# Rows of the second expert table gathered as 4 tokens x 32 slots, and summed by 32-column matmuls

## The chip, the cores and the metric

The kernel runs on one core of one Trainium2 chip. The metric is the device time of one execution in microseconds, as the median of several runs. Three runs of the kernel before gave 2932.99, 2933.3 and 2942.21 us, so the median is 2933.3 us.

## The reference, cut to what matters

The program computes three transformer blocks on one sequence of 256 tokens with 2048 channels, in 32-bit floating point. The change touches only one part, the expert layer at the end of the first block. For every token it picks 8 heads x 16 = 128 experts out of 16384, takes a dot product of the token with each expert's row of `expert_u`, and adds up the same experts' rows of `expert_v` with the resulting weights:

```
s1 = einsum('thd,nd->thn', q[:, :, 0], sk[0]); s2 = einsum(... q[:, :, 1], sk[1])
v1, i1 = top_k(s1, 16);  v2, i2 = top_k(s2, 16)
cs, ci = top_k(v1[..., :, None] + v2[..., None, :], 16)      # per token and head
experts = row * 128 + col;  gates = softmax(cs)
a = gelu(einsum('chkd,cd->chk', expert_u[experts], h))
out = einsum('chk,chkd->cd', gates * a, expert_v[experts])   # 128 rows per token
```

One row of either table is 2048 floats, 8 KB. 256 tokens x 128 experts x 2 tables are 65,536 rows, 512 MiB.

## The kernel before

Tokens lie on the 128 partitions, in two tiles t = 0 and 1. Outside the expert layer the program is a series of dense layers (`dense`): weights come in parts of 512 KB on SP's queue (`raw<-...`), ScalarE makes the high part of the split weight (`hi`, L110), VectorE the low part (`lo`, L111), and TensorE runs three matmuls per part and token tile (L178 to L180). `prep` keeps three parts (`LOOK`) ready ahead. ACT stands for ScalarE, DVE for VectorE, PE for TensorE, POOL for GpSimd and SP for SyncE.

The expert layer (`peer`) starts with the dense layer `w_qp`, 4 column blocks. After each block, `ev_qp` makes scores, and `route` finds the 16 best per head for two heads, that is 32 of the 128 expert slots of a token tile. It is some 40 small DVE instructions, written as a generator that runs a piece at each tick of the program. It ends with a cast of 32 expert numbers into `eidx` (L696). The four routes of t = 0 run inside and right behind `w_qp`; the scores of t = 1 wait in `sc1`, and its four routes (`late`) run beside the gathers.

Gathers are indirect DMAs that POOL issues (L740). One gather brings, for one slot k, the rows of 128 tokens, one on each partition: 128 x 8 KB = 1 MiB. Five buffers of that size go round: four of `gslot` and one in `hj`. The order written out by hand is a pair for each slot, first the u row, then the v row. In `step`, DVE takes the dot product of the u row with the tokens (L788, two instructions, 128x2048) and the buffer is free; ACT applies gelu and the gate (L790, L791). One slot later `vsum` uses the v row: ACT makes a diagonal matrix of the weights (`dg`, L764), PE multiplies it with the first 1024 columns of the row (L766, two matmuls of 512 columns, which the trace counts as four records of two passes each), and DVE adds the other 1024 columns, scaled, to `xres` (L767, "the half-sum"). When the 128 slots of a token tile are through, DVE adds the two PSUM accumulators to `xres` (L774), and `after_v` squares, transposes and splits the rows for the next layer, `ev_in`. Its first four weight parts are asked for 12 slots before the end.

Every 32-bit float matmul of 512 columns in this layer is two records on PE, each with a weight load of its own (PEld).

## Time and profile before

| what | value |
|---|---|
| median of three runs | 2933.3 us |
| the profiled execution | 2928.4 us, of which its span 2926.7 us |
| PE busy | 2349.1 us, 80% of the span |
| DVE busy | 1992.8 us, 68% |
| ACT, POOL busy | 1024.9 us (35%), 613.4 us (21%) |
| granted PE clock, mean | 0.876 of full speed |
| moved by gathers (queue software_dynamic) | 543.62 MB of 820.08 MB |
| gather stage, from the first gather to the last landing | 716.6 us to 2097.8 us |

The profiled execution's time is its span and 1.7 us around it. The page divides the span into 40 equal slices of 73 us; the stage of the gathers fills slices 10 to 28. Times within the program are counted from the start of the span. A queue or an engine is read as the bound of a stretch where it is busy throughout and the others wait for it.

### The profile page before, as it was taken

How to read it: one execution, taken by the hardware profiler on the slowest of the kernel's cores; microseconds unless marked ns; L12 is line 12 of the kernel's file. 1: busy time of each engine (PE TensorE's matmuls, PEld its weight loads, DVE VectorE, ACT ScalarE, POOL GpSimd, SP SyncE). 2: the span in 40 equal slices, each digit the busy share in tenths (PEclk: the TensorE clock that was granted, in tenths of full speed). 3: DMA queues.
4: the chain of work that ended last, by engine and by line, in shares of the span. 5: the costliest groups of instructions: out<-in, count | busy, mean ns of one | idle time of the engine just before them, and what ended most of it. 6: DMA issues, size and time to landing. Idle time of an engine off the chain costs nothing.

```text
span 2926.7 us, 25901 instructions
## 1 busy us (share of the span) xinstructions
PE 2349.1 (80%) x8448; PEld 1541.0 (53%) x8448; DVE 1992.8 (68%) x2705; ACT 1024.9 (35%) x1984; POOL 613.4 (21%) x569
## 2 busy tenths in 40 slices
PE   9999999999855555556655556565699999999999
PEld 7878888887511111111211111111388888888887
DVE  5665755657999767766766676667765566577754
ACT  6544544444422111111211111111344444446553
POOL 0000000000333444444444444444300000000000
PEclk9999999999965767786787677867899999999999
DMA  7545466556999999999999999999865555554345
GB/s 251 171 143 186 152 219 198 185 188 226 368 331 325 415 396 419 415 400 394 391 412 404 397 415 406 404 402 416 327 195 189 169 170 189 188 174 130 123 155 168
DMA packets 151912, 820.08 MB, mean 280 GB/s; under 512 B 17217, under 2 KB 17249, under 8 KB 85729
## 3 DMA queue, kind: packets, MB, share of 16 engines
q0 software_dynamic: 75312, 543.62, 46.6%
q1 hardware_dynamic: 76464, 274.81, 28.6%
q8 instruction: 67, 1.10, 0.2%
q14 instruction: 69, 0.56, 0.1%
HBM read 816.26 MB, written 2.10 MB: 280 GB/s over the span
## 4 chain that ended last, share of the span: by engine, by line
PE 48%; issue 18%; DMA 17%; POOL 8%; DVE 7%; ACT 1%; POOLq 0%; SPq 0%; DVEq 0%; ACTq 0%
PE acc L178 14%; PE acc L180 14%; PE acc L179 14%; DMA gslot<-expert_u,eidx 10%; POOL gslot L740 6%; DMA hj<-expert_u,eidx 5%; POOL hj L740 2%; DVE hj L788 2%; PE tr L207 1%; DVE lo L111 1%; DVE xres L767 1%; PE sd L1060 1%; PE sd L1069 1%; PE tr L284 1%; DMA xt<-xT 0%
## 5 line engine op out<-in xcount | busy, mean ns | idle before, releaser
L766 PE MATMUL acc<-gslot,dg 128*128 128x512 f32 x1024 | 769.8, 894 | 556.7 <-ACT dg L764 539.1
L111 DVE TENSOR_TENSOR lo<-raw,hi 128x1024 fp32r<-128x1024 f32 (+1 forms) x516 | 622.8, 1210 | 465.6 <-ACT hi L110 465.2
L766 PEld LDWEIGHTS acc<-gslot,dg 128*128 128x128 f32 x1024 | 242.1, 260 | 1075.8 <-ACT dg L764 873.6
L110 ACT ACTIVATE hi<-raw 128x1024 fp32r<-128x1024 f32 (+1 forms) x516 | 541.1, 1049 | 703.4 <-PE acc L180 628.3
L178 PE MATMUL acc<-hi,h 128*128 128x512 f32 (+1 forms) x1472 | 583.5, 397 | 3.7 <-ACT hi L110 3.3
L179 PE MATMUL acc<-lo,h 128*128 128x512 f32 (+1 forms) x1472 | 574.7, 390 | 4.5 <-DVE lo L111 4.5
L180 PE MATMUL acc<-hi,h 128*128 128x512 f32 (+1 forms) x1472 | 574.2, 390 | 0.8 <-DVE h L217 0.8
L767 DVE SCALAR_TENSOR_TENSOR xres<-gslot,wsl,xres 128x1024 f32<-128x1024 f32 x256 | 328.4, 1283 | 139.3 <-ACT wsl L791 125.6
L790 ACT ACTIVATE wsl<-dots 128x1 f32<-128x1 f32 x256 | 51.9, 203 | 1050.0 <-DVE dots L788 1050.0
L788 DVE CUSTOM_DVE_ANT_0 hj<-gslot,hj 128x2048 f16<-128x2048 f32 x129 | 295.5, 2291 | 111.6 <-DMA gslot<-expert_u,eidx 111.6
L788 DVE CUSTOM_DVE_ANT_0 hj<-hj 128x2048 f16<-128x2048 f32 x127 | 290.9, 2291 | 100.6 <-DMA hj<-expert_u,eidx 100.6
L740 POOL DMA_INDIRECT gslot<-expert_v,eidx x256 | 320.2, 1251 | 92.7 <-issue 75.8
L178 PEld LDWEIGHTS acc<-hi,h 128*128 128x128 f32 x1472 | 277.0, 188 | 67.4 <-issue 7.9
L179 PEld LDWEIGHTS acc<-lo,h 128*128 128x128 f32 x1472 | 277.5, 189 | 62.9 <-DVE lo L111 7.0
L180 PEld LDWEIGHTS acc<-hi,h 128*128 128x128 f32 x1472 | 277.2, 188 | 60.0 <-issue 1.6
L740 POOL DMA_INDIRECT gslot<-expert_u,eidx x129 | 127.8, 990 | 417.5 <-DVE dots L788 331.1
L195 POOL TENSOR_TENSOR rs_y<-rs_v,mhalf 128x2 f32<-128x2 f32 (+2 forms) x25 | 28.0, 1121 | 803.8 <-DVE rs_v L194 803.2
L740 POOL DMA_INDIRECT hj<-expert_u,eidx x127 | 123.1, 969 | 345.1 <-DVE dots L788 314.3
L764 ACT ACTIVATE dg<-ident,wsl 128x128 f32<-128x128 f32 x256 | 102.7, 401 | 8.4
L791 ACT ACTIVATE wsl<-wsl,gate 128x1 f32<-128x1 f32 x256 | 75.3, 294 | 8.2
L270 ACT ACTIVATE at<-at,sm_nm 128x128 f32<-128x128 f32 (+1 forms) x112 | 49.6, 444 | 40.4 <-DVE sm_nm L263 22.1
L178 PE MATMUL acc<-hi,mT 128*128 128x512 f32 x128 | 50.1, 392 | 0.0
(287 smaller groups left out, 2152.4 us busy)
## 6 DMA issues: line engine op xcount, KB each, us to landing
raw<-ev_in SPq DMA_DIRECT2D x128, 512.0 KB, 4.5
raw<-od_in SPq DMA_DIRECT2D x72, 512.0 KB, 3.8
raw<-w_gate SPq DMA_DIRECT2D x64, 512.0 KB, 4.0
raw<-w_dqkv SPq DMA_DIRECT2D x48, 512.0 KB, 3.6
raw<-w_out SPq DMA_DIRECT2D x32, 512.0 KB, 3.9
raw<-w_qp SPq DMA_DIRECT2D x32, 512.0 KB, 5.3
raw<-ev_out SPq DMA_DIRECT2D x32, 512.0 KB, 4.1
raw<-od_out SPq DMA_DIRECT2D x32, 512.0 KB, 4.4
```

The costliest lines, as they stand in the source:

```text
L110: nc.scalar.activation(hi, raw, AF.Copy)
L111: nc.vector.tensor_tensor(lo, raw, hi.bitcast(F32), op=ALU.subtract)
L178: nc.tensor.matmul(o, xh, wh, start=(k == 0), stop=False)
L179: nc.tensor.matmul(o, xh, wl, start=False, stop=False)
L180: nc.tensor.matmul(o, xl, wh, start=False, stop=(k == kc * kk - 1))
L740: nc.gpsimd.indirect_dma_start(out=g, out_offset=None, in_=d[table], in_offset=bass.IndirectOffsetOnAxis(ap=eidx[:, t, k:k + 1], axis=0))
L764: nc.scalar.activation(dg, self.ident, AF.Copy, scale=w)
L766: nc.tensor.matmul(st["acc"][n], dg, g[:, n * 512:(n + 1) * 512], start=(k == 0), stop=(k == P - 1))
L767: nc.vector.scalar_tensor_tensor(xres[:, t, VPE:], g[:, VPE:], w, xres[:, t, VPE:], op0=ALU.mult, op1=ALU.add)
L788: nc.vector.tensor_tensor_reduce(junk, gu, hrow[:, t], 1.0, 0.0, op0=ALU.mult, op1=ALU.add, accum_out=dots[:, t, o])
L790: nc.scalar.activation(wsl[:, t, o], dots[:, t, o], AF.Gelu_apprx_tanh)
L791: nc.scalar.activation(wsl[:, t, o], wsl[:, t, o], AF.Copy, scale=gate[:, t, o])
```

## The change

It replaces the way in which v rows are fetched, weighted and summed; u rows are fetched and used as before.

- A v gather now brings 4 tokens x 32 slots of one route block: partition 32m + r holds slot r of token 4i + m of a group q of 32 tokens. 32 such gathers cover the 128 tokens of a block. `spread` brings the expert numbers into that layout (`eidv`): a transpose on PE and four 32x32 casts on DVE, in each route.
- When 32 u slots are done, `weights` computes gelu and gate for all of them at once, transposes the weights with `spread`, and multiplies them with a constant mask into `lw`, 32 matrices of 128x32. So a v row needs four matmuls of 512 columns with 32 weight columns each, whose result goes to 32 of the 128 partitions of four PSUM accumulators. The diagonal, the half-sum and ACT's work for each slot are gone. `use_v` handles two v rows at a time.
- v rows run 36 places behind u rows (`VLAG`). The list of gathers begins with 36 u rows, goes on with u and v in turn, and ends with v rows alone.
- The two split-weight buffers `hi` and `lo` are one pool `hlp` of four buffers of 1 MiB. After `w_qp` all four also hold gathered rows (`hg`); within the last 16 uses they are given back, and only then are the first weight parts of `ev_in` asked for. One of the four `gslot` buffers holds the scores of t = 1 until they are routed. So four buffers go round at first, eight after `w_qp`, nine at the end.

```diff
-VPE = 1024
+VLAG = 36
...
-        self.hip = pool("hip", 4)
-        self.lop = pool("lop", 4)
+        self.hlp = pool("hlp", 4)
...
-        while self.nprep < min(upto, len(self.plan)):
+        while self.nprep < min(upto, self.limit, len(self.plan)):
             src, ks, n = self.plan[self.nprep]
             raw = self.rawp.tile([P, ks, n], F32, tag="raw", name="raw")
             nc.sync.dma_start(raw, src)
-            hi = self.hip.tile([P, ks, n], F32R, tag="hi", name="hi")
-            lo = self.lop.tile([P, ks, n], F32R, tag="lo", name="lo")
+            hl = self.hlp.tile([P, 2, ks, n], F32R, tag="hl", name="hl")
+            hi, lo = hl[:, 0], hl[:, 1]
...
-        base = [gslot[:, i] for i in range(4)] + [gbc]
-        free = deque(base)
-        ready = [[0, 0], [0, 0]]
+        sc1 = gslot[:, 3].rearrange("p (b c) -> p b c", b=4)
+        free = deque([(gslot[:, i], False) for i in range(3)] + [(gbc, False)])
+        ready = [0, 0]
...
+        def spread(dst, src, b, copy):
+            tp = self.tr()
+            nc.tensor.transpose(tp[:, :P], src, self.ident)
+            tv = tp[32 * b:32 * b + 32, :P].rearrange("p (i m) -> p m i", m=4)
+            for m in range(4):
+                copy(dst[32 * m:32 * m + 32], tv[:, m])
...
+            spread(eidv[:, t, sl], ef[:, t], b, nc.vector.tensor_copy)
...
+        seq = []
+        for j in range(256 + VLAG):
+            if j < 256:
+                seq.append(("u", j))
+            if j >= VLAG:
+                seq.append(("v", j - VLAG))
+        st = {"issue": 0, "use": 0, "acc": None, "keep": True, "gone": 0}
+        held, lws, pair = {}, {}, []
+
+        def vpos(v):
+            t, b, r = v // P, v // 32 % 4, v % 32
+            return t, b, r // 4, r % 4
...
+                kind, j = seq[st["issue"]]
+                if kind == "u":
+                    t, k = j // P, j % P
+                    if k >= ready[t]:
+                        return
+                    table, ix = "expert_u", eidx[:, t, k:k + 1]
+                else:
+                    t, b, i, q = vpos(j)
+                    c = 32 * b + 8 * q + i
+                    table, ix = "expert_v", eidv[:, t, c:c + 1]
+                g = free.popleft()
+                nc.gpsimd.indirect_dma_start(out=g[0], out_offset=None, in_=d[table],
+                                             in_offset=bass.IndirectOffsetOnAxis(ap=ix, axis=0))
+                held[kind, j] = g
...
-        def vsum(i, g):
-            t, k = todo[i]
-            w = wsl[:, t, k:k + 1]
-            if k == 0:
-                st["acc"] = [self.acc() for _ in range(2)]
-            dg = dgp.tile([P, P], F32, tag="dg", name="dg")
-            nc.scalar.activation(dg, self.ident, AF.Copy, scale=w)
-            for n in range(2):
-                nc.tensor.matmul(st["acc"][n], dg, g[:, n * 512:(n + 1) * 512], start=(k == 0), stop=(k == P - 1))
-            nc.vector.scalar_tensor_tensor(xres[:, t, VPE:], g[:, VPE:], w, xres[:, t, VPE:], op0=ALU.mult, op1=ALU.add)
-            free.append(g)
...
+        def weights(t, b):
+            sl = slice(32 * b, 32 * b + 32)
+            nc.scalar.activation(dots[:, t, sl], dots[:, t, sl], AF.Gelu_apprx_tanh)
+            nc.vector.tensor_tensor(dots[:, t, sl], dots[:, t, sl], gate[:, t, sl], op=ALU.mult)
+            yield 1
+            wT = self.small(32, "wT", bufs=2)
+            spread(wT, dots[:, t], b, lambda o, i: nc.scalar.activation(o, i, AF.Copy))
+            lw = pp.tile([P, 4, 8, 32], F32, tag="lw", name="lw", bufs=2)
+            nc.vector.tensor_tensor(lw, vmask.unsqueeze(1).to_broadcast([P, 4, 8, 32]),
+                                    wT.rearrange("p (g i) -> p g i", g=4).unsqueeze(3).to_broadcast([P, 4, 8, 32]), op=ALU.mult)
+            lws[t, b] = lw
...
+        def use_u(j):
+            t, k = j // P, j % P
+            g = held.pop(("u", j))
+            nc.vector.tensor_tensor_reduce(junk, g[0], hrow[:, t], 1.0, 0.0, op0=ALU.mult, op1=ALU.add,
+                                           accum_out=dots[:, t, k:k + 1])
+            give(g)
+            if k % 32 == 31:
+                self.spawn(weights(t, k // 32))
+
+        def use_v(v):
+            pair.append(v)
+            if len(pair) < 2:
+                return
+            gs = [held.pop(("v", x)) for x in pair]
+            if v % P == 1:
+                st["acc"] = [self.acc() for _ in range(4)]
+            for n in range(4):
+                for x, g in zip(pair, gs):
+                    t, b, i, q = vpos(x)
+                    nc.tensor.matmul(st["acc"][n][32 * q:32 * q + 32], lws[t, b][:, q, i], g[0][:, n * 512:(n + 1) * 512],
+                                     start=(x % P < 4), stop=(x % P >= P - 4))
+            pair.clear()
+            for g in gs:
+                give(g)
...
+            while st["use"] < len(seq):
+                kind, j = seq[st["use"]]
+                if (kind, j) not in held or (kind == "v" and vpos(j)[:2] not in lws):
+                    return
+                (use_u if kind == "u" else use_v)(j)
+                st["use"] += 1
+                fill()
+                if kind == "v" or j < VLAG:
+                    return
...
+        for _ in range(4):
+            free.append((self.hlp.tile([P, D], F32, tag="hl", name="hg"), True))
...
+            if st["keep"] and st["use"] >= len(seq) - 16:
+                st["keep"] = False
+                for g in [g for g in free if g[1]]:
+                    free.remove(g)
+                    st["gone"] += 1
+            if st["gone"] == 4:
+                st["gone"] = 0
+                self.limit = len(self.plan)
                 self.prep(self.ncons + 1 + LOOK)
```

In PE's program, in the middle of the stage of t = 0, `dg` is a slot's diagonal, `lw` a block's weight table; each row is one matmul of 512 columns, and the buffers of `gslot` all have one number. Before:

```order
L766 MATMUL acc_5891<-gslot_5352,dg_7546 128x512
L766 MATMUL acc_5892<-gslot_5352,dg_7546 128x512
L766 MATMUL acc_5891<-gslot_5352,dg_7556 128x512
L766 MATMUL acc_5892<-gslot_5352,dg_7556 128x512
L766 MATMUL acc_5891<-gslot_5352,dg_7566 128x512
L766 MATMUL acc_5892<-gslot_5352,dg_7566 128x512
L766 MATMUL acc_5891<-gslot_5352,dg_7576 128x512
L766 MATMUL acc_5892<-gslot_5352,dg_7576 128x512
```

And of the changed kernel, at the same place:

```order
L815 MATMUL acc_6317<-hg_5981,lw_6635 32x512
L815 MATMUL acc_6318<-hg_5981,lw_6635 32x512
L815 MATMUL acc_6319<-hg_5981,lw_6635 32x512
L815 MATMUL acc_6320<-hg_5981,lw_6635 32x512
L664 MATMUL tr_6864<-ident_84,dots_5119 128x128
L815 MATMUL acc_6317<-hg_5983,lw_6635 32x512
L815 MATMUL acc_6318<-hg_5983,lw_6635 32x512
L815 MATMUL acc_6319<-hg_5983,lw_6635 32x512
L815 MATMUL acc_6320<-hg_5983,lw_6635 32x512
```

Where two matmuls of a v row stood, four stand now, one after another on the same buffer (`hg_5981`, then `hg_5983`), and those of the next row follow. Matmuls of two rows in alternation stand only among the first few rows of the stage.

On DVE, in the same part of the stage, an ISA row of 128x2048 is a dot with a u row, and an ISA row of 128x1 reads its sum. Before:

```order
L767 SCALAR_TENSOR_TENSOR xres<-gslot,wsl,xres 128x1024
L788 ISA hj,dots<-hj 128x2048
L788 ISA dots 128x1
L767 SCALAR_TENSOR_TENSOR xres<-gslot,wsl,xres 128x1024
L788 ISA hj,dots<-gslot,hj 128x2048
L788 ISA dots 128x1
L767 SCALAR_TENSOR_TENSOR xres<-gslot,wsl,xres 128x1024
```

Changed:

```order
L799 ISA hj,dots<-gslot,hj 128x2048
L799 ISA dots 128x1
L787 TENSOR_TENSOR dots<-dots,gate 128x32
L792 TENSOR_TENSOR lw<-vmask,wT 128x1024
L799 ISA hj,dots<-gslot,hj 128x2048
L799 ISA dots 128x1
L799 ISA hj,dots<-hg,hj 128x2048
L799 ISA dots 128x1
L799 ISA hj,dots<-hg,hj 128x2048
L799 ISA dots 128x1
```

The half-sum between two dots is gone, and once in 32 dots two instructions for the weight table come in. Counted from the first dot, the last cast of expert numbers stood behind 32 dots and now stands behind 47.

On POOL, at the end of the gathers, each row is a gather of 1 MiB. Before:

```order
L740 DMA gslot<-expert_u,eidx 128x2048
L740 DMA gslot<-expert_v,eidx 128x2048
L740 DMA hj<-expert_u,eidx 128x2048
L740 DMA gslot<-expert_v,eidx 128x2048
L740 DMA gslot<-expert_u,eidx 128x2048
L740 DMA gslot<-expert_v,eidx 128x2048
```

Changed:

```order
L773 DMA hg<-expert_u,eidx 128x2048
L773 DMA gslot<-expert_v,eidv 128x2048
L773 DMA gslot<-expert_u,eidx 128x2048
L773 DMA gslot<-expert_v,eidv 128x2048
L773 DMA hj<-expert_v,eidv 128x2048
L773 DMA gslot<-expert_v,eidv 128x2048
L773 DMA hg<-expert_v,eidv 128x2048 x4
L773 DMA gslot<-expert_v,eidv 128x2048 x3
L773 DMA hj<-expert_v,eidv 128x2048
L773 DMA gslot<-expert_v,eidv 128x2048
```

The last u gather was the last but one of all, and is now followed by 37 v gathers.

## Rows read from the trace of the kernel before

**Rows 1.** The page: busy tenths and data rate in 40 slices.

```profile
PE   9999999999855555556655556565699999999999
...
DMA  7545466556999999999999999999865555554345
GB/s 251 171 143 186 152 219 198 185 188 226 368 331 325 415 396 419 415 400 394 391 412 404 397 415 406 404 402 416 327 195 189 169 170 189 188 174 130 123 155 168
```

**Rows 2.** Stretches: span; PE, PEld, DVE, ACT, POOL busy; PE clock, DMA share, GB/s.

```profile
716.60:948.00 231.40, 151.65 (x368) 73.40 (x366) 222.69 (x548) 70.79 (x145) 86.44 (x68) 0.72 0.93 342
948.00:2090.00 1142.00, 667.04 (x924) 214.11 (x924) 797.67 (x672) 203.54 (x675) 482.48 (x442) 0.74 1.00 406
1025.00:1050.00 25.00, 14.81 (x20) 4.22 (x18) 16.64 (x14) 3.74 (x13) 13.65 (x9) 0.64 0.99 384
1175.00:1200.00 25.00, 14.51 (x19) 4.75 (x20) 17.98 (x16) 4.49 (x15) 10.59 (x10) 0.70 1.01 420
```

**Rows 3.** Groups, 948 to 2090: busy us, mean ns, idle before and releaser.

```profile
L767 DVE SCALAR_TENSOR_TENSOR xres<-gslot,wsl,xres 128x1024 f32<-128x1024 f32 x221 | 283.8, 1284 | 137.5 <-ACT wsl L791 123.8 <-DMA gslot<-expert_v,eidx 9.6 <-ACT dg L764 4.1
L764 ACT ACTIVATE dg<-ident,wsl 128x128 f32<-128x128 f32 x221 | 88.7, 401 | 7.3
```

**Rows 4.** In order of time, three dots: start us, us, instruction, idle before it.

```profile
1335.82 2.29 DVE L788 CUSTOM_DVE_ANT_0 hj<-hj 128x2048 f16<-128x2048 f32 x1 [0.81 <-DMA hj<-expert_u,eidx]
1338.04 0.08 DVE L788 DVE_READ_ACCUMULATOR2_ANT dots<- 128x1 f32 x1
1338.39 0.94 POOL L740 DMA_INDIRECT hj<-expert_u,eidx  x1 [2.57 <-DVE dots L788]
1341.89 2.29 DVE L788 CUSTOM_DVE_ANT_0 hj<-gslot,hj 128x2048 f16<-128x2048 f32 x1 [1.88 <-DMA gslot<-expert_u,eidx]
1346.88 2.29 DVE L788 CUSTOM_DVE_ANT_0 hj<-hj 128x2048 f16<-128x2048 f32 x1 [0.81 <-DMA hj<-expert_u,eidx]
```

**Rows 5.** Gathers, 948 to 2090: POOL's wait, issue to landing.

```profile
  DVE dots L788: 582.3, 215
...
DMA to landing us min/median/max: 5.8/7.4/8.9
```

**Rows 6.** DVE's groups, 716.6 to 948.

```profile
L767 DVE SCALAR_TENSOR_TENSOR xres<-gslot,wsl,xres 128x1024 f32<-128x1024 f32 x32 | 40.8, 1274 | 0.0
L788 DVE CUSTOM_DVE_ANT_0 hj<-gslot,hj 128x2048 f16<-128x2048 f32 x17 | 38.7, 2278 | 5.7 <-DMA gslot<-expert_u,eidx 5.7
L111 DVE TENSOR_TENSOR lo<-raw,hi 128x1024 fp32r<-128x1024 f32 x16 | 19.4, 1209 | 1.3 <-ACT hi L110 1.3
```

**Rows 7.** Casts of expert numbers (ns, first and last start); two matmuls of w_qp.

```profile
L696 DVE CAST eidx<-rt_e x8: 152/174/182, 715.5 to 944.3; 128x32 uint32<-128x32 f32 x8
...
745.02 0.39 PE L178 MATMUL acc<-hi,h 128*128 128x512 f32 x1
745.25 0.39 PE L179 MATMUL acc<-lo,h 128*128 128x512 f32 x1
```

**Rows 8.** L766 on PE: in w_qp; three, four records at either clock; a load.

```profile
L766 PE MATMUL acc<-gslot,dg x24: 591/592/1221, 728.5 to 778.5; 128*128 128x512 f32 x24
...
1008.87 1.55 PE L766 MATMUL acc<-gslot,dg 128*128 128x512 f32 x3 [1.55 <-ACT dg L764]
1008.87 1.98 PE L766 MATMUL acc<-gslot,dg 128*128 128x512 f32 x4 [1.55 <-ACT dg L764]
1009.83 0.19 PEld L766 LDWEIGHTS acc<-gslot,dg 128*128 128x128 f32 x1 [0.24 <-issue]
1345.24 2.63 PE L766 MATMUL acc<-gslot,dg 128*128 128x512 f32 x3 [2.61 <-ACT dg L764]
1345.24 3.48 PE L766 MATMUL acc<-gslot,dg 128*128 128x512 f32 x4 [2.61 <-ACT dg L764]
```

**Rows 9.** The first addition of the sums at the end.

```profile
2102.36 0.69 DVE L774 TENSOR_TENSOR xres<-acc,xres 128x512 f32<-128x512 f32 x1 [0.35 <-PE acc L766]
```

**Rows 10.** A dense stretch, columns as in the stretches above.

```profile
2150.00:2250.00 100.00, 99.88 (x451) 81.99 (x450) 58.52 (x69) 42.55 (x44) 0.00 (x0) 1.00 0.57 186
```

More of the change, by code (lines that the diff above doesn't have):

```diff
@@ L736, in after_v @@
             self.row_to_lhs(xres[:, t, sl], h3[:, t, 0], h3[:, t, 1], 4 * b, 0, 4, fgain)
-        def gather(table, t, k):
-            g = free.popleft()
-            nc.gpsimd.indirect_dma_start(
-                out=g, out_offset=None, in_=d[table],
-                in_offset=bass.IndirectOffsetOnAxis(ap=eidx[:, t, k:k + 1], axis=0))
-            return g
-        todo = [(t, k) for t in range(2) for k in range(P)]
-        st = {"issue": 0, "dot": 0, "acc": None, "prev": None}
-        held = {}
@@ L749, in can @@
-        def can(i):
-            return i < len(todo) and todo[i][1] < ready[todo[i][0]][0]
-        def fill():
-            while free and can(st["issue"] // 2):
-                i, which = st["issue"] // 2, st["issue"] % 2
-                held[i, which] = gather(("expert_u", "expert_v")[which], *todo[i])
-                st["issue"] += 1
-        def vsum(i, g):
-            t, k = todo[i]
-            w = wsl[:, t, k:k + 1]
-            if k == 0:
-                st["acc"] = [self.acc() for _ in range(2)]
-            dg = dgp.tile([P, P], F32, tag="dg", name="dg")
-            nc.scalar.activation(dg, self.ident, AF.Copy, scale=w)
-            for n in range(2):
-                nc.tensor.matmul(st["acc"][n], dg, g[:, n * 512:(n + 1) * 512], start=(k == 0), stop=(k == P - 1))
-            nc.vector.scalar_tensor_tensor(xres[:, t, VPE:], g[:, VPE:], w, xres[:, t, VPE:], op0=ALU.mult, op1=ALU.add)
-            free.append(g)
-            if k == P - 1:
+        seq = []
@@ new lines, in peer @@
+        for j in range(256 + VLAG):
[8 more added lines that the diff above has]
+            return t, b, r // 4, r % 4
+        def fill():
+            while free and st["issue"] < len(seq):
+                kind, j = seq[st["issue"]]
[12 more added lines that the diff above has]
+                held[kind, j] = g
+                st["issue"] += 1
@@ new lines, in give @@
+        def give(g):
+            if st["keep"] or not g[1]:
+                free.append(g)
+            else:
+                st["gone"] += 1
[10 more added lines that the diff above has]
+            lws[t, b] = lw
@@ L770, in vsum @@
                 if t == 0:
                     self.h3.append(self.slot("B", [P, 2, 2, 16, P], F32R, name="h3"))
[L772 removed]
+                for n in range(4):
                     c = slice(n * 512, (n + 1) * 512)
                     nc.vector.tensor_tensor(xres[:, t, c], st["acc"][n], xres[:, t, c], op=ALU.add)
[L775 to L776 removed]
+                    self.spawn(after_v(n, t))
         def step():
             fill()
[L780 removed]
@@ L792, in step @@
-            free.append(gu)
-            st["dot"] += 1
-            if st["prev"] is not None:
-                vsum(st["prev"], held.pop((st["prev"], 1)))
-            st["prev"] = i
-            fill()
+            while st["use"] < len(seq):
[7 more added lines that the diff above has]
+                    return
@@ L808, in peer @@
         self.hook = None
-        late = [(b, 1) for b in range(4)]
-        while st["dot"] < len(todo):
-            if late and st["dot"] >= 20 and not any(x[3] == "late" for x in self.tasks) and ready[0][1] == P:
-                b, t = late.pop(0)
-                self.spawn(route(b, t, sc1[:, b]), "late")
+        for _ in range(4):
+            free.append((self.hlp.tile([P, D], F32, tag="hl", name="hg"), True))
+        late = [0, 1, 2, 3]
+        while st["use"] < len(seq):
+            if st["use"] >= 20 and ready[0] == P and not any(x[3] == "late" for x in self.tasks):
+                if late:
+                    b = late.pop(0)
+                    self.spawn(route(b, 1, sc1[:, b]), "late")
+                elif ready[1] == P and sc1 is not None:
+                    free.append((gslot[:, 3], False))
+                    sc1 = None
             self.tick()
             step()
-            if st["dot"] == len(todo) - 12:
+            if st["keep"] and st["use"] >= len(seq) - 16:
+                st["keep"] = False
+                for g in [g for g in free if g[1]]:
+                    free.remove(g)
+                    st["gone"] += 1
+            if st["gone"] == 4:
+                st["gone"] = 0
+                self.limit = len(self.plan)
                 self.prep(self.ncons + 1 + LOOK)
-        vsum(st["prev"], held.pop((st["prev"], 1)))
         self.flush()
@@ L1160, in consts @@
     out["kdec"] = np.ascontiguousarray((np.exp(lg[None, :] * (127.0 - i[:, None])) / 16.0).astype(f))
+    vm = np.zeros((4, 32, 8, 32), f)
+    for m in range(4):
+        for i_ in range(8):
+            vm[m, :, i_, 4 * i_ + m] = 1.0
+    out["vmask"] = vm.reshape(P, 8, 32)
     return out
```

33 lines of the change are left out of this document (10 added, 23 removed).

## Prediction

> **What bounds the kernel now.** I read the page first, then a table of stretches, then groups, then single instructions. In the page [rows 1] the reader should follow the DMA line: for some 18 of its 40 slices, from about 720 us on, it stands at 9 and the data rate near 400 GB/s, while PE falls to half. That is the expert stage, the only one the change rewrites. The slices before and after it, where PE stands at 9, keep their order and their waits, so I leave them out of the sum.
>
> The table of stretches [rows 2] splits the stage in two. From the first gather to the end of the routing (716.6 to 948) DVE is busy 222.7 of 231.4 us and the DMA moves 342 GB/s: DVE sets the end there. From 948 to 2090 the DMA engines' share is 1.00 at 406 GB/s and DVE has 344 us to spare: the transfers set the end. The groups of that second stretch [rows 3] count 221 pairs of gathers (the half-sum of L767 runs once a pair), so a pair takes 1142/221 = 5.17 us, a gather of 128 rows of 8 KB 2.584 us. Single instructions [rows 4] show what varies: one dot starts 4.99 us before the next, another 6.07 us before it; each u gather is issued right after a dot, and each dot waits for a landing. A gather lands 7.4 us after its issue [rows 5], which at 2.5 us each is three gathers on the way out of five buffers; POOL waits 215 times for a dot to give a buffer back, 582 us in all.
>
> **The change, in three stretches.**
>
> *Routing.* Here DVE's sum decides. Half-sums go: 32 x 1.274 = -40.8 us [rows 6]. But u rows now run ahead: by the order of DVE the last index cast stands behind 47 dots, before it was 32, so 15 dots more at 2.28 + 0.08 us [rows 4, 6] = +35.4. One weight table of 128x1024, like the splits of that shape, +1.2 [rows 6]; 28 casts of 32x32, not in the trace, at most like the 128x32 cast, 0.17 each, +4.9 [rows 7]. Together +0.7: nothing. The new casts also wait: each reads a transpose that stands in PE's queue, in w_qp behind matmuls of weight parts that DVE had prepared up to three parts earlier, 12 x 0.225 us each [rows 7]. Queued behind the cast on DVE are the next splits and the next dots. That is 0 to 8 us for each of two blocks in the projection; the later ones meet a nearly empty PE. I take 6 in all (bounds 0 and 16). The last cast, at 944.3 before [rows 7], comes at 951. By then 47 u and 11 v rows are used and 8 buffers issued: 66 gathers, against 32 + 31 + 5 = 68. DVE having been the bound, most of the 8 have landed; I count 64 down. PE loses six of its L766 groups inside w_qp, about 2 us each [rows 8], so the projection ends sooner; as DVE bounds this stretch, that is worth nothing.
>
> *Body.* The last u gather is number 476 of 512; 412 are still to land at 951. Bytes per gather are the same. DVE has one dot per pair, 2.4 of 5 us, POOL the same two issues of about 1 us, so the DMA stays the bound; what can change is its gaps. With eight buffers (nine once the second scores are routed) and less time held in each by DVE, some six gathers are on the way in place of three. Two windows of rows 2 show what a short queue costs: where nine issues took 13.65 us of POOL instead of ten in 10.59, the rate was 384 GB/s and not 420. Such holes should close. Best spacing 4.99 a pair gives 2.495 a gather, the present mean 2.584; those are the bounds, and I take 2.52, since the DMA share in the best window leaves nothing but landing hiccups. 412 x 2.52 = 1038: the last u lands at 1989 (before's spacing: 2016). The eight weight blocks make DVE wait for a gelu, a transpose behind one v row and four small copies, 3 to 6 us estimated from ACT's 0.4 us a copy and PE's 3.4 us a row [rows 3, 8]; six buffers on the way cover 15 us, so it costs nothing; without that cover, 8 x 4 = 32 us.
>
> *Tail.* The order of POOL ends in 37 v gathers with no u between them, and so does PE's work. A v row costs PE four matmuls of 512 columns, each two records, so 8 records where it was 4. The fourth record of a group adds 0.43 us at 2.4 GHz and 0.85 us at 1.2 GHz [rows 8]. PE's order shows the four matmuls of one row in a run, then the four of the next: they share a column group, so only the last record of one row can run beside the first of the next. That gives 8 x 0.43 = 3.44 us, or 3.01 with that overlap; I take 3.2, more than the 2.52 us a transfer takes. The Trainium skill, "TensorE: Matmul & The Clock Gate", Part 3, measured 2.38 times for three column tiles of 32 at 512 columns, and says beside it that matmuls start and end in program order. By the factor a row would cost 1.4 us and the tail would be the transfers'; by the order of starts only the seam overlaps. The rows at hand are of full-width matmuls and show neither. So PE, until now hidden by 5 us of transfer per pair, becomes the bound: 36 x 3.2 = 115 us, sums done at 1989 + 115 = 2104. Before, the first addition of the sums starts at 2102.4 [rows 9]. Four additions of 0.69 us stand where two stood, partly under the transposes: +1. Next stage +2.7 us. The first four weight parts of the next stage now wait for the row buffers to be given back, within the last 16 uses, some 50 us ahead of the end: 2 MB are 5 us of transfer, and the DMA has 36 x (3.2 - 2.52) = 24 us to spare there, with ACT and DVE idle for the splits. Nothing, as long as PE bounds the tail; +5 where the transfers do. ACT's work per pair (gelu, scale, diagonal, 0.9 us) goes too; nobody waits long for it once buffers abound.
>
> Sum against the profiled execution: 2928.4 + 2.7 = 2931. The median of the runs shown is 2933.3, 4.9 above the profiled one: **2936 us**. Bounds of the parts: routing -6/+10, body -10/+26, tail -7/+9; put together loosely 2921 to 2961.
>
> **The rivals.**
>
> *The column groups overlap fully.* For it: two neighbouring rows do write different 32-partition groups. Against it: a row's four matmuls stand in a run. If a v row cost PE no more than 2.52 us, the tail would be a transfer tail: 1989 + 36 x 2.52 + 3 = 2083, 21 us less: 2915 (2905 to 2925). This is what the skill's factor above comes to.
>
> *The deeper queue does nothing*, the slow gathers being the memory's own: body at 2.584, +26: 2962.
>
> *Weight loads come to light.* Now each is 0.19 us for 128 columns and runs under the previous matmul [rows 8]. If a load into the column group in use had to wait for the matmul, 8 x 0.19 = 1.5 us a row: 4.7 x 36 = 169, +54: 2990. Four times narrower loads would bring it to +14. The Trainium skill, same page, Part 3 (what overlaps), has a load run beside a matmul only where the row group differs; here all row groups are the same, so by it this rival holds. The trace of before disagrees for full-width weights: there loads start with the previous matmul though both use all rows [rows 8].
>
> *The clock stays low*, the slower side, from one mechanism: PE's granted clock averages 0.74 in this stage with PE 58% busy, and 1.00 where it is always busy [rows 2, 8, 10]. With 32 of 128 columns at work the clock may not be granted. At 1.2 GHz a row takes 8 x 0.85 = 6.8, or 5.95 with the seam; 256 rows from about 900 us (the 36th dot stands two routes before the last cast) end at 900 + 256 x 6.4 = 2538, +436: 3370. It decides where a record's mean exceeds 5.04/8 = 0.63 us. Against it: at the low clock PE would be busy without a pause, which in the dense stages goes with the full clock.
>
> That rows don't really travel in the split-weight buffers can be left out: they appear in POOL's order until the last gathers.
>
> **How the numbers follow.** My sum 0.45, full overlap 0.25, no help from depth 0.10, loads exposed 0.11, low clock 0.09. About 0.3% (9 us) is what a measurement of this kernel can tell from no change. Of the sum's 0.45, 0.30 lies within it, 0.05 below, 0.10 above; of full overlap 0.22 below and 0.03 within; the others are slower. Faster 0.27, same 0.33, slower 0.40. The range leaves out the low clock and half of the exposed loads: 2908 to 2980.
>
> **What would show it.** In the profile after: the last index cast near 951 with DVE busy up to there; pairs of dots 5.04 us apart and a rate of 416 GB/s in the body; PE busy 3.0 to 3.4 us a v row at the full clock; some 115 us between the last dot and the additions, with the DMA share under 1. Wrong would make it: v matmuls of one row starting side by side, granted clock at 0.5 in the body, PE ahead of the landings in the tail, or a body at 406 GB/s as before.

## The result, and the profile after

| kernel | median, us | ratio to before, 95% interval |
|---|---|---|
| before | 2933.0 | 1 |
| changed | 2911.9 | 0.9925 [0.9907, 0.9942] |

The change made the kernel 0.75% faster, 21 us, where I had forecast 2936 us, next to no change, and had held slower (0.40) likelier than faster (0.27). The time lies inside the range, at its lower end, and nearest to the first rival (2915).

The page of the changed kernel, in the lines of [rows 1] and the granted clock:

```profile
PE   9999999999506777777777777778999999999999
...
PEclk9999999999758999999999999999999999999999
DMA  7545466556878999999999999999755555553345
GB/s 253 170 145 182 153 218 199 187 189 214 328 269 336 400 420 420 420 420 420 420 420 420 420 420 420 421 420 420 305 187 190 170 171 186 189 177 129 123 154 168
```

Two things are to be seen. From the fifteenth slice on the rate stands at 420 GB/s without a gap, where it wandered between 391 and 419 before. But the eleventh to fourteenth slices read 328, 269, 336, 400 where before they read 368, 331, 325, 415: the first part of the stage got worse. The stretches say the same (columns as in [rows 2]):

```profile
716.10:948.00 231.90, 98.52 (x336) 52.68 (x334) 217.06 (x569) 25.20 (x38) 100.64 (x65) 0.71 0.83 314
948.00:1990.00 1042.00, 759.95 (x1691) 169.73 (x1692) 498.99 (x450) 12.14 (x47) 487.24 (x419) 0.99 1.01 419
1990.00:2086.00 96.00, 95.36 (x298) 27.96 (x297) 7.32 (x9) 6.11 (x9) 26.81 (x29) 0.99 0.97 399
```

342 GB/s fell to 314 in the lead (up to 948), 406 rose to 419 in the body, and a third stretch, the tail of v rows alone, runs at 399. The gathers of the body (POOL's wait for a dot, and issue to landing, as in [rows 5]):

```profile
  DVE dots L799: 15.5, 4
...
DMA to landing us min/median/max: 7.5/18.5/19.5
```

POOL hardly waits for dots any more, and a gather takes 18.5 us to land in place of 7.4: at 2.5 us each that is seven on the way in place of three. Single instructions of the body, in order of time, as in [rows 4]:

```profile
1398.68 2.29 DVE L799 CUSTOM_DVE_ANT_0 hj<-gslot,hj 128x2048 f16<-128x2048 f32 x1 [2.69 <-DMA gslot<-expert_u,eidx]
...
1401.08 3.62 PE L815 MATMUL acc<-gslot,lw 128*32 128x512 f32 x8 [1.35 <-DMA gslot<-expert_v,eidv]
...
1403.67 2.29 DVE L799 CUSTOM_DVE_ANT_0 hj<-gslot,hj 128x2048 f16<-128x2048 f32 x1 [2.69 <-DMA gslot<-expert_u,eidx]
```

Almost every dot starts 4.99 us after the last, as only the best did before; the mean over the body is 5.01. A v row alone takes PE eight records, 3.62 us: seven steps of 0.43 and the last record's own 0.6, as the sum had it, so no weight load came to light. Last, the index casts, and the first addition of the sums at the end ([rows 7] and [rows 9] before):

```profile
L704 DVE CAST eidx<-ef x8: 154/164/332, 715.1 to 948.4; 128x32 uint32<-128x32 f32 x8
...
2083.25 1.42 DVE L826 TENSOR_TENSOR xres<-acc,xres 128x512 f32<-128x512 f32 x2 [30.30 <-PE acc L815]
```

The last cast came 4 us later than before, the additions 19 us earlier.

**The tail.** Here the prediction went wrong. PE at its beginning, in order of time:

```profile
1987.66 0.30 PE L664 MATMUL tr<-ident,dots 128*128 128x128 f32 x1 [1.90 <-DVE dots L787]
1987.89 4.03 PE L815 MATMUL acc<-gslot,lw 128*32 128x512 f32 x5
1991.24 0.68 PE L815 MATMUL acc<-hj,lw 128*32 128x512 f32 x1
1991.75 0.59 PE L815 MATMUL acc<-gslot,lw 128*32 128x512 f32 x1
1991.76 0.59 PE L815 MATMUL acc<-hj,lw 128*32 128x512 f32 x1
1992.18 0.59 PE L815 MATMUL acc<-gslot,lw 128*32 128x512 f32 x1
1992.19 0.59 PE L815 MATMUL acc<-hj,lw 128*32 128x512 f32 x1
1992.61 0.59 PE L815 MATMUL acc<-gslot,lw 128*32 128x512 f32 x1
1992.62 1.02 PE L815 MATMUL acc<-hj,lw 128*32 128x512 f32 x2
1993.05 0.62 PE L815 MATMUL acc<-gslot,lw 128*32 128x512 f32 x1
...
1994.80 0.62 PE L815 MATMUL acc<-hg,lw 128*32 128x512 f32 x1
```

In the program these rows stand one behind another, four matmuls each:

```
L664 MATMUL tr_8092<-ident_84,dots_5119 128x128
L815 MATMUL acc_7423<-gslot_5127,lw_7863 32x512
L815 MATMUL acc_7424<-gslot_5127,lw_7863 32x512
L815 MATMUL acc_7425<-gslot_5127,lw_7863 32x512
L815 MATMUL acc_7426<-gslot_5127,lw_7863 32x512
L815 MATMUL acc_7423<-hj_5123,lw_7863 32x512
```

Yet the first record of the `hj` row starts at 1991.24, with the fifth record of the `gslot` row, and the two rows go on in pairs, 0.01 us apart. With rows in store one starts 1.78 us after another (1991.24, 1993.05, 1994.80): half of 8 x 0.43. That is less than the 2.5 us of a transfer. So once the store is used up PE waits for landings, 2.49 us from row to row, which the weight loads near the end show; where the first four weight parts of the next stage (`raw`) take their share of the DMA, it is 3.8:

```profile
2045.49 7.81 SPq L106 DMA_DIRECT2D raw<-ev_in  x4
```

```profile
2057.03 0.14 PEld L815 LDWEIGHTS acc<-gslot,lw 128*32 128x32 f32 x2 [1.07 <-DMA gslot<-expert_v,eidv]
...
2060.80 0.14 PEld L815 LDWEIGHTS acc<-hj,lw 128*32 128x32 f32 x2 [1.06 <-DMA hj<-expert_v,eidv]
...
2064.59 0.14 PEld L815 LDWEIGHTS acc<-gslot,lw 128*32 128x32 f32 x2 [1.08 <-DMA gslot<-expert_v,eidv]
...
2067.08 0.22 PEld L815 LDWEIGHTS acc<-gslot,lw 128*32 128x32 f32 x3 [0.21 <-DMA gslot<-expert_v,eidv]
...
2069.57 0.22 PEld L815 LDWEIGHTS acc<-gslot,lw 128*32 128x32 f32 x3 [0.21 <-DMA gslot<-expert_v,eidv]
...
2072.06 0.22 PEld L815 LDWEIGHTS acc<-gslot,lw 128*32 128x32 f32 x3 [0.21 <-DMA gslot<-expert_v,eidv]
```

So the tail adds up from transfers alone. 37 rows at 2.495 us are 92.3, the 2.1 MB of weight parts at 420 GB/s are 5.0, and from the start of the last row (2082.04) to the first addition it is 1.2: 98.5 us from the last dot (1984.7).

### The profile page after: what moved, and what is told of

Same layout as the page of the kernel before. It is cut to its first block, busy times and chain, and to the rows that moved or that the text cites. A ratio compares the mean times of both kernels' runs of the same rounds, so it can differ in the third digit from the quotient of the medians.

```text
span 2910.2 us, 26316 instructions
## 1 busy us (share of the span) xinstructions
PE 2481.5 (85%) x9488; PEld 1506.8 (52%) x9488; DVE 1687.2 (58%) x2503; ACT 790.4 (27%) x1244; POOL 657.0 (23%) x570
## 4 chain that ended last, share of the span: by engine, by line
PE 53%; DMA 35%; DVE 5%; issue 4%; POOL 2%; ACT 0%; SPq 0%; POOLq 0%; DVEq 0%; ACTq 0%
PE acc L177 15%; PE acc L178 15%; PE acc L179 15%; DMA gslot<-expert_v,eidv 14%; DMA hg<-expert_v,eidv 14%; DMA hj<-expert_v,eidv 5%; PE acc L815 3%; POOL gslot L773 2%; DMA gslot<-expert_u,eidx 2%; DVE hj L799 2%; PE tr L206 1%; PE sd L1114 1%; PE sd L1123 1%; PE tr L283 1%; DVE hl L110 1%
## 5 line engine op out<-in xcount | busy, mean ns | idle before, releaser
L110 DVE TENSOR_TENSOR hl<-raw,hl 128x1024 fp32r<-128x1024 f32 (+1 forms) x516 | 623.1, 1210 | 521.9 <-ACT hl L109 521.4
L109 ACT ACTIVATE hl<-raw 128x1024 fp32r<-128x1024 f32 (+1 forms) x516 | 541.2, 1050 | 758.2 <-PE acc L179 613.8
L177 PE MATMUL acc<-hl,h 128*128 128x512 f32 (+1 forms) x1472 | 581.9, 396 | 3.1 <-ACT hl L109 3.1
L178 PE MATMUL acc<-hl,h 128*128 128x512 f32 (+1 forms) x1472 | 574.1, 390 | 6.6 <-DVE hl L110 6.6
L179 PE MATMUL acc<-hl,h 128*128 128x512 f32 (+1 forms) x1472 | 573.3, 389 | 0.0
L815 PE MATMUL acc<-gslot,lw 128*32 128x512 f32 x880 | 393.0, 601 | 123.7 <-DMA gslot<-expert_v,eidv 123.5
L815 PE MATMUL acc<-hg,lw 128*32 128x512 f32 x864 | 379.3, 608 | 124.1 <-DMA hg<-expert_v,eidv 121.7
L799 DVE CUSTOM_DVE_ANT_0 hj<-hg,hj 128x2048 f16<-128x2048 f32 x115 | 263.5, 2291 | 238.9 <-DMA hg<-expert_u,eidx 238.7
L177 PEld LDWEIGHTS acc<-hl,h 128*128 128x128 f32 x1472 | 277.4, 189 | 65.0 <-issue 6.6
L178 PEld LDWEIGHTS acc<-hl,h 128*128 128x128 f32 x1472 | 277.4, 188 | 64.5 <-DVE hl L110 10.3
L179 PEld LDWEIGHTS acc<-hl,h 128*128 128x128 f32 x1472 | 277.2, 188 | 57.5 <-issue 0.3
L773 POOL DMA_INDIRECT hg<-expert_u,eidx x115 | 155.0, 1348 | 278.1 <-PE acc L815 65.6
L815 PE MATMUL acc<-hj,lw 128*32 128x512 f32 x304 | 145.1, 623 | 45.1 <-DMA hj<-expert_v,eidv 45.1
L773 POOL DMA_INDIRECT gslot<-expert_v,eidv x110 | 111.9, 1017 | 79.2 <-issue 27.1
```

The lines of the kernel that those rows point to most:

```text
L109: nc.scalar.activation(hi, raw, AF.Copy)
L110: nc.vector.tensor_tensor(lo, raw, hi.bitcast(F32), op=ALU.subtract)
L177: nc.tensor.matmul(o, xh, wh, start=(k == 0), stop=False)
L178: nc.tensor.matmul(o, xh, wl, start=False, stop=False)
L179: nc.tensor.matmul(o, xl, wh, start=False, stop=(k == kc * kk - 1))
L773: nc.gpsimd.indirect_dma_start(out=g[0], out_offset=None, in_=d[table], in_offset=bass.IndirectOffsetOnAxis(ap=ix, axis=0))
```

## The experiments

Two questions lead: is the tail's pace due to the column groups, and why is the whole gain 21 us when the body alone went from 406 to 419 GB/s? Medians of before in these runs are 2930 to 2931 us, in the result above 2933.0, so differences between kernels of different rounds are good to some 3 us.

**Depth alone, and the layout alone.** `b_deep` is the kernel before with one pool for both split weights, whose four buffers hold rows after w_qp; `a_shallow` is the changed kernel without them.

```diff
 b_deep, against the kernel before
-        self.hip = pool("hip", 4)
-        self.lop = pool("lop", 4)
+        self.hlp = pool("hlp", 4)
...
+        for _ in range(4):
+            hgs.append(self.hlp.tile([P, D], F32, tag="hl", name="hg"))
+            free.append(hgs[-1])
...

 a_shallow, against the changed kernel
-        for _ in range(4):
-            free.append((self.hlp.tile([P, D], F32, tag="hl", name="hg"), True))
...
```

> The kernel before, with nothing of the change but the pooled split-weight buffers: nine row buffers after w_qp in place of five, u and v rows and sums as before. Theory 1 (the body's gain of 0.09 us a gather comes from the deeper queue alone): some 440 gathers at 2.495 in place of 2.584 us, 39 us less, so about 2893 us, faster than the changed kernel, since the lead keeps 342 GB/s and there is no tail. Rival (the gaps came from DVE's half-sums and ACT's work per slot, or from the way v rows were gathered): the body stays at 406 GB/s, 2928 to 2935 us.

> The changed kernel without the four row buffers from the split-weight pool: four buffers, five once the second scores are routed. Theory 1 (depth): a gather again 2.58 us or more, since a v row holds its buffer 3.6 us on PE: 412 x 0.09 = 37 us or more in the body, 2950 to 2985 us, and fewer than four gathers on the way. Rival (the layout and the lighter DVE closed the gaps): 419 GB/s as in the changed kernel, 2912 to 2920 us.

Measured: `b_deep` 2889.7 us, ratio 0.9861 [0.9843, 0.9879]; `a_shallow` 2954.3 us, 1.009 [1.007, 1.011]. Theory 1 holds in both. The stretches of `b_deep`, and its gathers in the body:

```profile
716.00:948.00 232.00, 152.97 (x379) 76.70 (x378) 221.67 (x549) 69.42 (x146) 105.28 (x74) 0.73 0.93 356
948.00:2050.00 1102.00, 636.58 (x924) 202.87 (x922) 799.00 (x675) 206.62 (x676) 538.71 (x437) 0.77 1.01 417
```

```profile
DMA to landing us min/median/max: 7.3/18.2/19.8
```

And of `a_shallow`:

```profile
716.00:948.00 232.00, 94.90 (x322) 52.19 (x321) 219.71 (x575) 29.20 (x42) 87.35 (x57) 0.68 0.79 291
948.00:2000.00 1052.00, 758.63 (x1657) 168.28 (x1655) 483.94 (x433) 11.19 (x42) 470.57 (x409) 0.98 1.00 407
```

```profile
  DVE dots L799: 334.6, 102
...
DMA to landing us min/median/max: 5.8/8.5/10.4
```

The body's rate goes with the buffers, not with the layout: 406 and 407 with five, 417 and 419 with nine, whether DVE does a half-sum in each pair or not. The four kernels make a table that adds up. More buffers give 41 us under the old layout (2930.4 to 2889.7) and 42 under the new (2954.3 to 2911.9). The new layout costs 24 us with few buffers and 22 with many. So the new layout (four tokens in a gather, column tiles, v rows 36 places behind) is a loss; the change is faster because of the buffers that came with it.

**Column groups in the tail.** `a_samegroup` takes v rows in an order in which eight rows running write one 32-partition group.

```diff
-            return t, b, r // 4, r % 4
+            return t, b, r % 8, r // 8
...
-                                     start=(x % P < 4), stop=(x % P >= P - 4))
+                                     start=(b == 0 and i == 0), stop=(b == 3 and i == 7))
```

> The changed kernel with v rows in another order: eight rows running write the same 32-partition group, then eight the next. Theory 1 (the tail came out at the transfers' pace because the next row's matmuls, in another column group, start while the row before still has four records to go): without another group a row costs PE 8 x 0.43 = 3.44 us, the last 36 rows 116 to 124 us in place of 96, so 2935 to 2942 us, as my prediction's own sum had it. Rival (PE overlaps any two rows, or is not what sets the tail): 2912 us.

Measured: 2932.2 us, ratio 1.0012 [1.0, 1.0024], 20 us above the changed kernel, where 23 to 30 were expected; the first addition of the sums starts at 2103.47 in place of 2083.25. PE in the tail, where one group ends (`gslot`) and the next begins (`hg`):

```profile
2047.41 3.60 PE L815 MATMUL acc<-hj,lw 128*32 128x512 f32 x8
2050.85 2.31 PE L815 MATMUL acc<-gslot,lw 128*32 128x512 f32 x5
2052.57 0.62 PE L815 MATMUL acc<-hg,lw 128*32 128x512 f32 x1
2052.99 0.59 PE L815 MATMUL acc<-gslot,lw 128*32 128x512 f32 x1
2053.02 0.59 PE L815 MATMUL acc<-hg,lw 128*32 128x512 f32 x1
```

Rows of one group follow each other 3.44 us apart without overlap (2047.41, 2050.85). At the seam the next row starts 1.72 us after the last, four records ahead. The whole tail, in the columns of [rows 2] with PE and PEld alone:

```profile
1985.40:2106.20 120.80, 120.47 (x296) 31.08 (x296) 1.00 0.85 325
```

Theory 1 holds: 37 rows at 3.44 us less 1.72 for each of four seams are 120.4 us, and PE is busy for 120.47. So the tail that I had predicted exists, but only for rows of one group. Without the seams it would have been 7 us longer, and the miss below the expected 23 us is theirs.

`a_double` does each matmul of a v row twice.

```diff
-                    nc.tensor.matmul(st["acc"][n][32 * q:32 * q + 32], lws[t, b][:, q, i], g[0][:, n * 512:(n + 1) * 512],
-                                     start=(x % P < 4), stop=(x % P >= P - 4))
+                    for w in range(2):
+                        nc.tensor.matmul(st["acc"][n][32 * q:32 * q + 32], lws[t, b][:, q, i], g[0][:, n * 512:(n + 1) * 512],
+                                         start=(x % P < 4 and w == 0), stop=(x % P >= P - 4 and w == 1))
```

> The changed kernel with each matmul of a v row done twice, so each v row counts twice in the sums: 16 records a row. Theory 1 (only the next row's start overlaps, some four records deep): a row costs 12 x 0.43 = 5.2 us or more, over the 5.0 us that a pair of transfers takes; PE bounds the stage from the first v row on, 256 x 5.2 = 1330 us from about 880, about 3030 us. Rival A (half of the work overlaps whatever its length): 3.44 us a row, hidden in the body, the tail 36 x 3.44 = 124 us: about 2940 us. Rival B (the four groups run beside each other freely): 2912 us.

Measured: 2985.9 us, ratio 1.0192 [1.0174, 1.0211]: between theory 1 (3030) and rival A (2940), and none of the three as written. In the tail:

```profile
2020.00:2160.00 140.00, 140.00 (x517) 39.95 (x516) 6.37 (x7) 5.67 (x8) 23.06 (x25) 1.00 0.62 216
```

517 records in 140 us are 4.33 us a row of 16, always busy. My theory took the matmuls of a row to stand in a run. In this kernel's PE program two of four rows do so, and the other two alternate in pieces. The starts of three rows show it: last a row in a run (`hj`) and the row behind it, and first the row four places before that one:

```profile
2068.11 0.62 PE L816 MATMUL acc<-gslot,lw 128*32 128x512 f32 x1
...
2080.21 0.62 PE L816 MATMUL acc<-hj,lw 128*32 128x512 f32 x1
...
2085.39 0.62 PE L816 MATMUL acc<-gslot,lw 128*32 128x512 f32 x1
```

The row after a row in a run starts 5.18 us behind it (2080.21, 2085.39): 12 x 0.43, as theory 1 had it, four records ahead once more. Four rows take 17.28 us (2068.11 to 2085.39), two runs of 5.18 and 6.9 for the pair that alternates, in which most records stand beside one of the other group. So the arithmetic of theory 1 holds, rival A is out, and the time missed by the order of PE's program: the body keeps the transfers' 419 GB/s, and 37 rows at 4.33 make a tail of 160 us where the changed kernel has 98.5. The groups don't run freely either (rival B): 16 records on one of four groups would then cost 1.7 us a row and hide.

**Where the layout loses its 22 us.** By the rows of both kernels it is the lead: 314 against 356 GB/s for 232 us is 9.7 MB, at 420 GB/s 23 us. Most of it stands early. The changed kernel, and then `b_deep`:

```profile
740.00:830.00 90.00, 30.66 (x132) 23.88 (x130) 87.93 (x230) 10.21 (x16) 35.46 (x23) 0.66 0.81 304
```

```profile
740.00:830.00 90.00, 66.81 (x218) 41.00 (x218) 85.77 (x200) 30.94 (x64) 40.83 (x30) 0.82 0.99 401
830.00:948.00 118.00, 65.44 (x74) 20.27 (x73) 117.62 (x308) 28.01 (x67) 55.25 (x36) 0.62 0.88 322
```

304 against 401 GB/s for 90 us are 8.7 MB, 21 us, while from 830 to 948 it is 310 against 322. DVE is busy 87.9 of the 90 us, so waits for transposes, or the one row buffer that the changed kernel has less than `b_deep`, can explain little of it. `a_lag64` makes the part with u rows alone longer.

```diff
-VLAG = 36
+VLAG = 64
...
-            lw = pp.tile([P, 4, 8, 32], F32, tag="lw", name="lw", bufs=2)
+            lw = pp.tile([P, 4, 8, 32], F32, tag="lw", name="lw", bufs=3)
```

> The changed kernel with v rows 64 places behind u rows in place of 36 (three weight tables in place of two). Theory 1 (the lead lands fewer gathers because u rows alone pass through DVE): the 11 v rows that came before the last index cast don't come there any more, 11 x 2.495 = 27 us later at the end: about 2939 us; the tail of 64 v rows stays at the transfers' pace. Rival (where u and v rows stand is all one): 2912 us. If the tail's rows were PE's, 28 more of them would add some 28 x 0.7 = 20 us on top of either.

Measured: 2926.8 us, ratio 0.9982 [0.9964, 1.0], 15 us above the changed kernel. The sign is theory 1's, the size half of it. The stretch 830 to 948 of the changed kernel and then of `a_lag64`:

```profile
830.00:948.00 118.00, 44.98 (x92) 9.89 (x92) 110.81 (x292) 5.74 (x12) 56.67 (x36) 0.69 0.83 310
```

```profile
830.00:948.00 118.00, 1.81 (x4) 0.73 (x4) 117.76 (x299) 5.36 (x12) 52.83 (x32) 0.50 0.76 272
```

38 GB/s for 118 us and another 38 up to 1000 us (392 against 354) are 6.5 MB, 15 us: the whole difference lies there. A tail of 64 v rows, 28 more, cost nothing besides. The shorter lag that would bring v rows in before 830 us was not tried.

If the lead is DVE's, moving the four late routes into the body, where DVE is idle half of the time, should give it back. The first attempt slowed their pieces: every second tick (`a_late`, begun at the 36th use; `b_deep_late`; `b_late` with five buffers), then every fourth (`a_late4`, `b_deep_late4`). The edit of `a_late`:

```diff
-        def route(b, t, sc):
+        def route(b, t, sc, gap=1):
...
-                yield 1
+                yield gap
...
-            if st["use"] >= 20 and ready[0] == P and not any(x[3] == "late" for x in self.tasks):
+            if st["use"] >= 36 and ready[0] == P and not any(x[3] == "late" for x in self.tasks):
...
...
-                    self.spawn(route(b, 1, sc1[:, b]), "late")
+                    self.spawn(route(b, 1, sc1[:, b], 2), "late")
```

> The changed kernel with the four late routes begun at the 36th use in place of the 20th and at half the pace (one piece every second tick). Theory 1 (what the column tiling loses against the kernel before with nine buffers, 22 us, is lost in the lead, where DVE, with routing pieces between dots of u rows alone, lands 314 GB/s where 420 are to be had): with the routing moved behind the first v rows, where DVE is half idle, the transfers set the end from about 800 us on: 40 to 55 us less, 2857 to 2872 us. Rival (the loss is elsewhere: the waits for the transposes of the index spread, or the tail): 2900 to 2912 us.

> The kernel before with nine row buffers, and the four late routes at half the pace. Theory 1: from 840 to 930 us its data rate is about 310 GB/s because of the routing on DVE; spread out, 420: 90 x 110 GB/s = 10 MB, 24 us less, about 2866 us, so that the difference to the changed kernel with the same edit nearly goes. Rival (with a half-sum in each pair DVE has no room for the routing in the body either: 3.65 + half of 2.2 us a pair under 5.0): 2880 to 2890 us.

> The kernel before, five buffers, with the late routes at half the pace, to see whether the two edits add up. Theory 1 (the lead is a loss of its own, apart from depth): the lead rises from 325 to 406 GB/s between 800 and 948 us: 12 MB, 25 to 30 us less, 2902 to 2908 us. Rival (with five buffers a routing piece between two dots holds a buffer back wherever it stands, so the loss only moves): 2920 to 2932 us.

> As the run before of the changed kernel with its late routes begun at the 36th use, now one piece every fourth tick. Theory 1 (with one piece every second tick DVE was still busy 100 per cent up to 948 us and the rate fell to 315 to 326 GB/s between 900 and 948; a pair takes 5.0 us of transfer, a dot 2.36 and at this pace some 0.6 us of routing): 420 GB/s from about 845 us on, so some 70 us x 90 GB/s = 6 MB, 15 us less than the 2894.9 of that run: about 2880 us. Rival (all that DVE has to do for routing is lost to the transfers wherever it stands): 2895 us.

> As the run before of the kernel before with nine buffers and slower late routes, now one piece every fourth tick. Theory 1 (at half the pace DVE was still full, 3.65 us for dot and half-sum and 1.2 of routing in a pair of 5.0; at a quarter it has 0.7 us a pair to spare): 405 GB/s or more from 840 us on in place of 315, 20 to 27 us less, 2863 to 2870 us. Rival (the DVE's work up to the last route is what it is, so spreading it only moves the loss): 2887 to 2891 us. Against the changed kernel with the same edit this tells what the column tiling is worth once routing no longer starves the transfers: I expect the two within 15 us.

Measured: `a_late` 2894.9 us (0.9883 [0.9847, 0.9919]), `b_deep_late` 2890.7 (0.9866 [0.9829, 0.9902]), `b_late` 2931.3 (1.0002 [0.9986, 1.0017]), `a_late4` 2895.0 (0.988 [0.986, 0.9899]), `b_deep_late4` 2887.4 (0.9852 [0.9832, 0.9872]). `a_late` gained 17 us, between what theory and rival had; the kernels before gained nothing clear, and the slower pace nothing more: on the time alone the rival has the four others. The rows show why that decides little. In `a_late4`:

```profile
830.00:948.00 118.00, 62.44 (x123) 13.87 (x124) 112.20 (x300) 4.45 (x11) 61.05 (x42) 0.80 0.91 358
```

DVE still runs 300 instructions there, as many as without the edit (292), though the last cast came only at 1334.0 us. The scheduler that writes each engine's order moves pieces that depend on nothing ahead, so most of the routing had not left the lead. What was gained stands in the same stretch: 358 against 310 GB/s are 5.7 MB, 13 us of the 17, with 123 records of v rows where there were 92. In the second attempt the pieces can't be moved: the scores of each late route are multiplied by a one that is made from a dot product (of `a_spread`; `b_spread` has the same with dots 30, 52, 74 and 96).

```diff
-                if late:
+                if late and st["use"] >= 44 + 32 * late[0]:
                     b = late.pop(0)
+                    one = self.small(1, "one")
+                    k = 40 + 16 * b
+                    nc.vector.tensor_scalar(one, dots[:, 0, k - 1:k], 0.0, 1.0, op0=ALU.mult, op1=ALU.add)
+                    nc.scalar.activation(sc1[:, b], sc1[:, b], AF.Copy, scale=one)
                     self.spawn(route(b, 1, sc1[:, b]), "late")
...
```

> The changed kernel; each late route's scores are first multiplied by one, made from a dot product, so that its pieces can't be moved ahead of dots 40, 56, 72 and 88 (slower pieces alone were still moved forward: 315 to 349 GB/s and DVE full between 900 and 948 us). Theory 1 (the lead's loss is DVE's routing standing before dots): 405 to 420 GB/s from 830 us on; until 1000 us that is 12 MB more than in the changed kernel, 29 us: 2883 us, up to 2893 if each burst of 20 us of routing outlasts the 15 us of rows that are on the way. Rival (what DVE has to do before the body is lost wherever it stands): 2895 us or more, dips of the rate behind each burst.

> The kernel before with nine row buffers, its late routes held in the same way behind dots 30, 52, 74 and 96. Theory 1: 10 MB more between 840 and 1000 us than with nine buffers alone, 24 us: about 2866 us, up to 2878 with what the bursts cost, so that the lead it shares with the changed kernel is the one place left to gain. Rival (a pair has 1.35 us of DVE to spare, too little to catch up within 22 pairs, so the loss only moves): 2885 to 2891 us.

Measured: `a_spread` 2883.6 us, ratio 0.9838 [0.9825, 0.9852]; `b_spread` 2866.1 us, 0.9779 [0.9765, 0.9792]. Both came where theory 1 had them. Two stretches of the lead, of `a_spread` and then of `b_spread`:

```profile
740.00:830.00 90.00, 29.38 (x133) 22.56 (x131) 88.16 (x212) 11.58 (x17) 36.54 (x24) 0.68 0.83 316
830.00:948.00 118.00, 65.96 (x146) 14.73 (x146) 90.40 (x135) 3.20 (x8) 78.63 (x50) 0.84 0.99 406
```

```profile
740.00:830.00 90.00, 66.61 (x216) 40.33 (x215) 86.05 (x198) 31.63 (x64) 40.56 (x30) 0.82 1.00 402
830.00:948.00 118.00, 70.32 (x103) 21.92 (x101) 104.05 (x144) 25.76 (x79) 53.81 (x50) 0.75 1.01 416
```

DVE's instructions between 830 and 948 fall to 135 and 144, and the rate rises from 310 and 322 GB/s to 406 and 416. That is worth 28 us in the new layout (2911.9 to 2883.6) and 24 in the old (2889.7 to 2866.1), so it is a loss that both share and not the layout's own. What still parts the two, 17 us, is the stretch 740 to 830: 86 GB/s for 90 us are 7.7 MB, 18 us. There DVE is full in both, and the kernel with u rows alone needs 2.36 us of DVE for each MiB, the other 3.64 for two.

## Why the prediction was wrong

*Routing.* The cast was forecast at 951 and came at 948.4: right. That 64 gathers would have landed was too many. The last dot starts at 1984.7; the 1036 us in between, at 2.50, are 414 gathers, so some 61 of 475 had landed (37 follow the last u gather, so it is number 475 and not 476). About 3 fewer of those issued were down than I counted; with one less in all, 2 more were to go, 5 us.

*Body.* The spacing was taken as 2.52 us; it measured 2.495, the lower bound, between most dots and 2.50 in the mean: some 7 us less. That the short queue made the gaps is shown by `b_deep` and `a_shallow`. With the earlier cast, the last u landing was forecast for 1989 and measured 1984.7. The eight weight blocks cost nothing, as said.

*Tail.* This is the step that failed: "they share a column group, so only the last record of one row can run beside the first of the next", from which 3.2 us a v row and 115 us followed. From the last u landing to the first addition it took 98.5 us. Between rows of different groups four of eight records overlap, which gives PE 1.78 us a row, and the transfers set the pace at 2.49. With that the weight parts, put at nothing "as long as PE bounds the tail; +5 where the transfers do", came to the 5 us. That the same arithmetic holds where the groups are equal is shown by `a_samegroup`. On the Trainium skill, "TensorE: Matmul & The Clock Gate", Part 3, which I weighed there: its gain from column tiles was the better guide, and its rule that matmuls start in program order is not what this trace shows, where the next row's first record starts with the fifth of the row before (1991.24). The size here, 3.44/1.78, is 1.93 times, from two groups at a time; no run here shows 2.38. I had taken the rule's side where rows of full-width matmuls could not show either, and gave the rival 0.25.

*Next stage.* From the first addition to the end 827.0 us, before 824.3: 2.7 more, where +1 was in the sum; what the rest is stays open.

*Rivals.* Deeper queue no help: refuted by `b_deep`. Exposed loads: 3.62 us for eight records, none. Low clock: 0.99 in the body, refuted. Full overlap: right that the transfers set the tail; as a mechanism it is half right, since four records overlap and not the row, as `a_samegroup` and `a_double` show. That its 2083 met the measured 2083.25 is in part luck: the body ended 4 us sooner, and the weight parts took 5 more. (In the rival of the low clock 2538 is 434 behind 2104, not 436.)

The forecast thus missed by 24 us: 16.5 in the tail (115 to 98.5), 4 ahead of it, and 5 that I had added because the median of before lay 4.9 above its profiled execution, where the changed kernel's does not; the next stage took 2 back. What the prediction left out altogether is that the two halves of the change pull apart: it priced the lead against the kernel before (two gathers fewer), and not against what eight buffers would have given under the old order.

## What to carry to other kernels

When a change bundles an enabling edit (freed memory, more buffers) with a rewrite, price and run each half alone: here the buffers gave 41 us and the rewrite took some 22 back. An engine that is idle half of a stage can still starve it at the beginning; ask which work stands there only because it was ready early, and tie it to something later, since asking for it later doesn't hold it back. The version that follows is the kernel before with nine buffers and held-back late routes, 2866.1 us, 2.2% under before and 1.6% under the changed kernel.

## What the runs showed of the hardware that I had not expected

- Rows for different column groups overlap though the program has them one behind the other: row starts 1.78 us apart, against 3.44 in one group. Four records ahead is what these traces show at every seam looked at where PE did not wait, with rows of eight records and of sixteen (5.18 us).
- The granted clock was 0.99 in the body (2.4 GHz nearly throughout) with matmuls of 32 columns that kept PE busy 760 of 1042 us, and 0.74 before with 128 columns and 667 of 1142. I had feared the opposite. What sets it was not tried.
- Seven gathers on the way in place of three brought only 3% more rate, but all of the gaps went: spacing 4.99 us a pair almost throughout, landing time 18.5 us in place of 7.4.
